# Storing the last tile of a streaming silu-multiply in two pieces of 4 rows instead of four of 2

## The chip, the cores and the metric

The kernel runs on one core of one Trainium2 chip. The metric is device microseconds (us) of one execution; lower is better.

## The reference, cut to what matters

```python
x = randn(32, 512, 2048) float32          # 16384 rows of 2048
x1, x2 = x[..., :1024], x[..., 1024:]
out = (x1 * (1 / (1 + exp(-x1)))) * x2    # silu of one half, times the other half
```

134.22 MB are read and 67.11 MB written.

## The kernel before

There are 16 tiles, numbered 0 to 15 here. A tile is 1024 rows of the input: each of the 128 partitions holds 8 consecutive rows (8 MB in, 4 MB out). Loads are issued by the scalar engine (ACT), stores by the sync engine (SP), so each kind has a queue of its own, and both queues are served by the same 16 DMA engines. An engine moves a transfer in packets; here a packet is the contiguous run of one partition, 64 KB in a load and 32 KB in a store of 8 rows. A queue is said to have drained, or run dry, when the last packet in it is done. Input and output tiles are double-buffered. Compute goes 2 rows at a time: ACT does the silu, the vector engine (DVE) the product.

```python
K = 8                  # rows per partition in a tile
KC = 2                 # rows per compute step
# ...
for i in range(n_tiles):
    # ...
    last = i == n_tiles - 1
    for c in range(0, k, KC):
        ce = min(c + KC, k)
        nc.scalar.activation(out=ot[:, c:ce, :], in_=xt[:, c:ce, :half], func=Silu)
        nc.vector.tensor_mul(out=ot[:, c:ce, :], in0=ot[:, c:ce, :], in1=xt[:, c:ce, half:])
        if last:                                                     # tile 15: one store per step
            nc.sync.dma_start(out=ov[:, c:ce, :], in_=ot[:, c:ce, :])
    if not last:                                                     # tiles 0..14: one store of 8 rows
        nc.sync.dma_start(out=ov, in_=ot[:, :k, :])
    if i + 2 < n_tiles:
        load(i + 2)
```

Of the kernel before, what the change touches and what calls it, by code (L numbers as in the profile page):

```python
# [1 line left out]

# [4 lines left out]


def issue_ahead_of_the_first_barrier(nc):




    head, body = nc.main_func.blocks[:2]
    load = next(ins for ins in body.instructions if type(ins).__name__ == "InstDMACopy")
    at = next(
        j for j, ins in enumerate(head.instructions)
        if ins.engine == load.engine and type(ins).__name__ == "InstDrain"
    )
    body.instructions = [ins for ins in body.instructions if ins.name != load.name]  # L20
    head.instructions = head.instructions[:at] + [load] + head.instructions[at:]


@with_exitstack
def kernel(
    ctx: ExitStack,
    tc: tile.TileContext,
    x: bass.AP,
    out: bass.AP,
):  # L30






    nc = tc.nc
    P = nc.NUM_PARTITIONS

    x_flat = x.flatten_outer_dims()  # L40
    out_flat = out.flatten_outer_dims()
    num_rows, in_cols = x_flat.shape
    half = in_cols // 2
    dt = x_flat.dtype

    K = 8
    KC = 2
    PLAN = [K] * (num_rows // (P * K))

    in_pool = ctx.enter_context(tc.tile_pool(name="in_pool", bufs=2))  # L50
    out_pool = ctx.enter_context(tc.tile_pool(name="out_pool", bufs=2))

    plan = []
    row = 0
    for k in PLAN:
        plan.append((row, k))
        row += P * k
    assert row == num_rows
    n_tiles = len(plan)

    def view(flat, i):
        row0, k = plan[i]
        return flat[row0:row0 + P * k].rearrange("(p k) d -> p k d", k=k)

    nc.at_finalize(issue_ahead_of_the_first_barrier)


    ctx.enter_context(tc.manual_schedule())

    loaded = {}  # L70

    def load(i):
        xt = in_pool.tile([P, K, in_cols], dt, name="xt")
        nc.scalar.dma_start(out=xt[:, :plan[i][1], :], in_=view(x_flat, i))
        loaded[i] = xt

    load(0)
    load(1)
    for i in range(n_tiles):
        k = plan[i][1]  # L80
        xt = loaded.pop(i)
        last = i == n_tiles - 1
        ov = view(out_flat, i)
        ot = out_pool.tile([P, K, half], dt, name="ot")
        for c in range(0, k, KC):
            ce = min(c + KC, k)
            nc.scalar.activation(  # L87
                out=ot[:, c:ce, :],
                in_=xt[:, c:ce, :half],
                func=mybir.ActivationFunctionType.Silu,  # L90
            )
            nc.vector.tensor_mul(  # L92
                out=ot[:, c:ce, :],
                in0=ot[:, c:ce, :],
                in1=xt[:, c:ce, half:],
            )
            if last:
                nc.sync.dma_start(out=ov[:, c:ce, :], in_=ot[:, c:ce, :])
        if not last:
            nc.sync.dma_start(out=ov, in_=ot[:, :k, :])  # L100
        if i + 2 < n_tiles:
            load(i + 2)


# [1 line left out]
_INS = ['x']  # L106
_OUTS = [((32, 512, 1024), 'float32')]


# [23 lines left out]
```

## Time and profile before

| | |
|---|---|
| time before, first three runs | 470.78 us (470.76 to 470.87) |
| span in the profile | 468.9 us |
| moved | 201.35 MB, mean 429 GB/s |
| DVE, ACT busy | 30%, 25% |
| last tile: multiplies end | 455.26, 457.46, 459.67, 461.87 us |
| last tile: stores issued | 455.29, 457.49, 459.69, 461.89 us |
| last data on the DMA engines | 467.62 us |

The page of the kernel before, its totals, the DMA row (busy tenths in 40 slices of the span) and the chain that ended last:

```profile
span 468.9 us, 269 instructions
DVE 142.3 (30%) x64; ACT 118.2 (25%) x65; POOL 0.2 (0%) x4
...
DMA  9899999999999998999999999999999989999998
...
DMA 80%; DVE 15%; ACT 3%; DVEq 0%; issue 0%
```

The DMA engines are at least 80% busy in every slice: they are the bottleneck. Compute appears in the chain because a new load waits for its buffer to be computed, but another load and a store are moving meanwhile.

The end is what the change touches. The timeline of the kernel before (start, duration, engine, line, operation; SPq is the sync engine's queue):

```profile
451.03 7.31 ACT L87 ACTIVATE ot<-xt 128x2048 f32<-128x2048 f32 x4 [21.57 <-DMA xt<-in_x_dram]
452.97 8.90 DVE L92 TENSOR_TENSOR ot<-ot,xt 128x2048 f32<-128x2048 f32 x4 [19.98 <-ACT ot L87]
455.29 6.94 SPq L98 DMA_DIRECT2D out_dram<-ot  x4
```

The four stores of line 98, and the time from issue to landing (minimum, median, maximum):

```profile
L98 SPq DMA_DIRECT2D out_dram<-ot x4: 332/332/333, 455.3 to 461.9; - x4
...
DMA to landing us min/median/max: 5.4/5.7/6.1
```

The windows of the kernel before over its end; the columns to read are the last two, the mean share of the 16 DMA engines and the rate. A packet is counted whole in the window in which it starts, so where packets are as long as the window the shares are lumpy and can exceed 1:

```profile
core 0: us, DVE busy (x) ACT busy (x) POOL busy (x), PEclk, DMA share, GB/s
...
455.00:457.00 2.00, 2.00 (x2) 2.00 (x2) 0.00 (x0) 1.00 0.68 295
457.00:457.50 0.50, 0.50 (x2) 0.50 (x1) 0.00 (x0) 1.00 0.87 361
457.50:458.00 0.50, 0.50 (x1) 0.50 (x1) 0.00 (x0) 1.00 0.97 410
458.00:458.50 0.50, 0.50 (x1) 0.34 (x1) 0.00 (x0) 1.00 1.04 442
458.50:459.00 0.50, 0.50 (x1) 0.00 (x0) 0.00 (x0) 1.00 0.93 393
459.00:467.30 8.30, 2.87 (x2) 0.00 (x0) 0.00 (x0) 1.00 0.97 408
467.30:468.90 1.60, 0.00 (x0) 0.00 (x0) 0.00 (x0) 1.00 0.01 5
```

The engines stay busy from the first small store to the last byte. The trace also records each DMA packet with its start, duration, size and queue. It explains the first two rows: until 457.00 (fastest engine) to 457.81 (slowest) the engines are still moving the whole-tile store of tile 14, in packets of 32 KB and 1.21 us. The first packet of the last tile starts some 3 ns later, on each engine, after a 4-byte completion packet. (The records do not name the engine, but packets of a busy engine follow one another so closely that 16 chains can be told apart.) That store was issued at 455.29, so 1.7 us of its life went by in a queue that was not empty. Its issue costs nothing.

### The profile page before, as it was taken

How to read it: one execution, taken by the hardware profiler on the slowest of the kernel's cores; microseconds unless marked ns; L12 is line 12 of the kernel's file. 1: busy time of each engine (PE TensorE's matmuls, PEld its weight loads, DVE VectorE, ACT ScalarE, POOL GpSimd, SP SyncE). 2: the span in 40 equal slices, each digit the busy share in tenths (PEclk: the TensorE clock that was granted, in tenths of full speed). 3: DMA queues.
4: the chain of work that ended last, by engine and by line, in shares of the span. 5: the costliest groups of instructions: out<-in, count | busy, mean ns of one | idle time of the engine just before them, and what ended most of it. 6: DMA issues, size and time to landing. Idle time of an engine off the chain costs nothing.

```text
span 468.9 us, 269 instructions
## 1 busy us (share of the span) xinstructions
DVE 142.3 (30%) x64; ACT 118.2 (25%) x65; POOL 0.2 (0%) x4
## 2 busy tenths in 40 slices
DVE  0070705106061160601507025070250702407034
ACT  1142406023060330603206032060420604106051
POOL 0000000000000000000000000000000000000000
DMA  9899999999999998999999999999999989999998
GB/s 431 375 447 403 447 447 447 403 419 431 447 447 403 447 492 363 442 492 391 458 403 439 456 447 403 409 442 447 447 403 444 467 386 447 442 419 481 400 409 354
DMA packets 5042, 201.35 MB, mean 429 GB/s; under 512 B 560, under 2 KB 560, under 8 KB 560
## 3 DMA queue, kind: packets, MB, share of 16 engines
q10 hardware_dynamic: 2304, 134.22, 66.4%
q1 hardware_dynamic: 2736, 67.11, 33.2%
q14 instruction: 2, 0.02, 0.0%
HBM read 134.22 MB, written 67.11 MB: 429 GB/s over the span
## 4 chain that ended last, share of the span: by engine, by line
DMA 80%; DVE 15%; ACT 3%; DVEq 0%; issue 0%
DMA xt<-in_x_dram 80%; DVE ot L92 15%; ACT ot L87 3%; DVEq L128 0%
## 5 line engine op out<-in xcount | busy, mean ns | idle before, releaser
L92 DVE TENSOR_TENSOR ot<-ot,xt 128x2048 f32<-128x2048 f32 x64 | 142.3, 2286 | 319.5 <-ACT ot L87 319.5
L87 ACT ACTIVATE ot<-xt 128x2048 f32<-128x2048 f32 x64 | 116.9, 1897 | 338.8 <-DMA xt<-in_x_dram 338.8
L87 ACT ACT_TABLE_LOAD x1 | 1.3, 1283 | 1.3 <-PEq L117 1.3
L117 POOL MEMSET const-uint8-127<- 128x1 uint8 x1 | 0.1, 102 | 0.0
L117 POOL MEMSET const-bfloat16-1.0<- 128x1 bf16 x1 | 0.1, 101 | 0.0
L117 POOL MEMSET const-float32-0.0<- 128x1 f32 x1 | 0.1, 98 | 0.2 <-issue 0.2
L117 POOL MEMSET const-float32-1.0<- 128x1 f32 x1 | 0.1, 98 | 0.0
## 6 DMA issues: line engine op xcount, KB each, us to landing
out_dram<-ot SPq DMA_DIRECT2D x15, 4096.0 KB, 39.8
out_dram<-ot SPq DMA_DIRECT2D x4, 1024.0 KB, 5.7
xt<-in_x_dram ACTq DMA_DIRECT2D x16, 47.1
```

What stands on the lines that cost most here:

```text
L87: nc.scalar.activation(out=ot[:, c:ce, :], in_=xt[:, c:ce, :half], func=mybir.ActivationFunctionType.Silu,)
L92: nc.vector.tensor_mul(out=ot[:, c:ce, :], in0=ot[:, c:ce, :], in1=xt[:, c:ce, half:],)
L117: nc = _bacc.Bacc("TRN2", target_bir_lowering=False, num_devices=1)
```

## The change

The intent is fewer and larger stores: two of 2 MB in place of four of 1 MB. Two issues and two completions fall away, and the contiguous run per partition grows from 8 KB to 16 KB. The computation is untouched.

```diff
     K = 8
     KC = 2
+    KS = 4
@@
-            if last:
-                nc.sync.dma_start(out=ov[:, c:ce, :], in_=ot[:, c:ce, :])
+            if last and ce % KS == 0:
+                nc.sync.dma_start(out=ov[:, ce - KS:ce, :], in_=ot[:, ce - KS:ce, :])
```

## The prediction

> **What bounds the kernel.** Memory traffic. The page's totals give 201.35 MB at 429 GB/s over a span of 468.9 us; its DMA row shows 9 or 8 tenths in every slice; DVE is busy 30%, ACT 25%. The chain of waits is 80% load, and the compute in it (1.92 us ACT, then 8.91 us DVE per tile) runs beside other transfers. The change touches only the end.
>
> **The end, before.** Timeline and store line: the last tile's load is consumed at 451.03; its four multiplies of 2.29 us end 2.20 us apart; each releases a 1 MB store, issued at 455.29, 457.49, 459.69 and 461.89 (0.33 us each). Packet records: tile 14's whole-tile store still has packets in the store queue until 457.0 on the fastest DMA engine and 457.8 on the slowest. The first small store's packets start 0.01 us behind them on each engine: its issue is entirely hidden. From then on the engines have no gap until 467.62 (windows: DMA share 0.97 to 0.98 from 457.5 to 467.3): 32 packets of 8 KB per engine, 0.306 us apart, 9.81 us. The sync queue's wait ends at 467.98 and the closing barrier takes 0.9 us. So the tail is bound by DMA throughput, not by when the last multiply ends.
>
> The Trainium skill, "DMA: Bandwidth & Descriptors", section "Queues, rings and completion order", says that each DMA engine consumes descriptors in ring order; the trace agrees, the last tile's packets following tile 14's.
>
> **What the change does.** The first store of the last tile waits for two multiplies: issue at 457.49 instead of 455.29. The last half's store goes at 461.89 as before. Two issues of 0.33 us vanish from the sync queue, which is idle: worth nothing. Packets become 16 KB instead of 8 KB, 256 instead of 512. From the records, 32 KB packets follow each other every 1.209 us (27.1 B/ns), 8 KB ones every 0.306 us (26.8 B/ns); 16 KB ones should take 0.609 us, 16 per engine 9.74 us: 0.07 us gained.
>
> **What lies on the critical path.** The slack that hides the first issue is smaller than 2.20 us. Issue to first packet was 1.01 us for the very first load (engines idle), most engines within 0.26 us of the first; the first small store bounds it at 1.71 us, since its packets were there by then. So piece one starts at 458.5 to 459.2, where the store queue ran dry at 457.0 to 457.8: the slowest engine idles some 0.7 to 1.5 us. Piece two, issued at 461.89, is queued by 463.6 at the latest, and piece one lasts until about 463.4 to 464, so no second gap, or a tiny one. The end moves by the gap less 0.07 us: about +0.9 us, all in the last slice.
>
> Predicted: 471.7 us, 8 times in 10 between 471.0 and 472.7. Faster by over 2%: 0.01; within 2%: 0.98; slower by over 2%: 0.01.
>
> **What would show it.** Two stores on the store line, issued near 457.5 and 461.9; windows with DMA share well under 1 between about 457.2 and 458.8 (before: 0.87 to 0.98); then gapless until about 468.4; 16 KB packets of about 0.61 us; everything before 455 unchanged.
>
> **What would make it wrong.** A shorter issue latency, or tile 14's store ending later, so nothing is lost; 16 KB packets distinctly faster; longer set-up for the larger store; a second gap before piece two; or earlier stages interleaving differently by some tenths of a per cent, which would drown 0.9 us.

## The result, and the profile after

| | before | after |
|---|---|---|
| median of 6 runs | 470.89 us | 471.53 us |
| lowest to highest | 470.76 to 471.38 | 471.31 to 471.74 |
| span in the profile | 468.87 us | 469.54 us |
| first small store issued | 455.29 | 457.57 |
| its first packet | 457.00 | 458.40 |
| last data on the DMA engines | 467.62 | 468.40 |

The ratio is 1.0012 with a 95% interval of 0.9999 to 1.0025: the same by the 2% rule, and by the times alone barely told from 1. A ratio here is the mean time of one kernel's fast runs over that of the other's of the same rounds, so it is not quite the ratio of the medians quoted. The difference of the medians is 0.64 us.

The page after:

```profile
span 469.5 us, 265 instructions
DVE 142.3 (30%) x64; ACT 118.2 (25%) x65; POOL 0.2 (0%) x4
...
DMA  9999999999999998999999999999999999999998
...
DMA 80%; DVE 15%; ACT 3%; DVEq 0%; issue 0%
```

Nothing shows at this scale. The timeline after, and its store line:

```profile
451.11 7.31 ACT L88 ACTIVATE ot<-xt 128x2048 f32<-128x2048 f32 x4 [21.18 <-DMA xt<-in_x_dram]
453.05 8.90 DVE L93 TENSOR_TENSOR ot<-ot,xt 128x2048 f32<-128x2048 f32 x4 [19.59 <-ACT ot L88]
457.57 4.74 SPq L99 DMA_DIRECT2D out_dram<-ot  x2
```

```profile
L99 SPq DMA_DIRECT2D out_dram<-ot x2: 332/332/332, 457.6 to 462.0; - x2
...
DMA to landing us min/median/max: 6.3/6.6/6.8
```

Compute starts within 0.08 us of where it did, and the first store is issued 2.28 us later. The windows after:

```profile
core 0: us, DVE busy (x) ACT busy (x) POOL busy (x), PEclk, DMA share, GB/s
...
455.00:457.00 2.00, 2.00 (x2) 2.00 (x2) 0.00 (x0) 1.00 0.87 377
457.00:457.50 0.50, 0.50 (x2) 0.50 (x1) 0.00 (x0) 1.00 0.01 0
457.50:458.00 0.50, 0.50 (x2) 0.50 (x1) 0.00 (x0) 1.00 0.01 0
458.00:458.50 0.50, 0.50 (x1) 0.42 (x1) 0.00 (x0) 1.00 1.00 426
458.50:459.00 0.50, 0.50 (x1) 0.00 (x0) 0.00 (x0) 1.00 0.23 98
459.00:467.30 8.30, 2.94 (x2) 0.00 (x0) 0.00 (x0) 1.00 1.04 442
467.30:468.90 1.60, 0.00 (x0) 0.00 (x0) 0.00 (x0) 1.00 0.39 164
```

From 457.0 to 458.0 no data packet starts: the shares that were 0.87 and 0.97 are 0.01. (The 0.23 in the fifth row is only lumpiness: the packets of 0.61 us that started just before 458.5 are counted in the row above.) By the packet records tile 14's store ends at 457.11 to 457.89, and the first packets of the last tile start together at 458.40 to 458.55. Each engine has a hole of between 0.51 us (last end to first start) and 1.44 us (first end to last start). Across a hole the 16 chains cannot be told apart: holes per engine are bounds. The tail's work, about 9.8 us per engine, is nearly unchanged but starts later, and it is what 467.30 to 468.90 now contains.

The two profiles account for the difference of 0.67 us in the span. The first issue came 2.28 us later (2.20 by the change, 0.08 because the last load happened to land later in this run). The time from the first issue to the last data shrank by 1.51 us, from 12.34 to 10.83 us: the last engine to start waited 0.98 us from the issue to its first packet where it had been 2.53 us, and its transfer took 0.04 us longer. The close-out, from the last data to the end of the span, shrank from 1.25 to 1.14 us. The sum is 2.28 - 1.51 - 0.11 = 0.66 us, the rest rounding.

### The profile page after: what moved, and what is told of

It reads as the page before. It is cut to its first block, busy times and chain, and to the rows that moved or that the text cites. A ratio compares the mean times of both kernels' runs of the same rounds, so it can differ in the third digit from the quotient of the medians.

```text
span 469.5 us, 265 instructions
## 1 busy us (share of the span) xinstructions
DVE 142.3 (30%) x64; ACT 118.2 (25%) x65; POOL 0.2 (0%) x4
## 4 chain that ended last, share of the span: by engine, by line
DMA 80%; DVE 15%; ACT 3%; DVEq 0%; issue 0%
DMA xt<-in_x_dram 80%; DVE ot L93 15%; ACT ot L88 3%; DVEq L129 0%
```

## The experiments

The theory to be tested, called the gap theory: the DMA engines bind the tail, so a late issue costs exactly what exceeds the time for which the store queue is still busy. The rivals: the size of the stores or packets costs the time; the larger last store costs it; or the 0.64 us is drift. All times are medians; "over before" is the difference to the median of before. Kernels are compared only within the same rounds.

| run | last tile's stores (rows) | over before, us | 95% interval of the ratio |
|---|---|---|---|
| e0_after | 4, 4 | +0.61 | 0.9999 to 1.0024 |
| e1_late4 (failed to delay) | 2, 2, 2, 2 | -0.30 | 0.9984 to 1.0009 |
| e9_late4_held | 2, 2, 2, 2, in pairs | +0.63 | 0.9998 to 1.0023 |
| e2_422 | 4, 2, 2 | +0.94 | 1.0007 to 1.0034 |
| e3_224 | 2, 2, 4 | +0.04 | 0.9988 to 1.0013 |
| e4_62 | 6, 2 | +2.77 | 1.0045 to 1.0072 |
| e5_8 | 8 | +4.94 | 1.0091 to 1.0118 |
| e10_26 | 2, 6 | +2.37 | 1.0035 to 1.0063 |
| e6_rows1_ks4 | 4, 4, computed by single rows | +0.06 | 0.9992 to 1.0017 |
| e7_prev_small | 4, 4, tile 14 in 2-row stores | +0.30 | 0.9993 to 1.0018 |
| e7b_prev_small_2222 | 2, 2, 2, 2, tile 14 likewise | +0.31 | 0.9991 to 1.0016 |
| e8_rows1_ks1 | eight of 1, computed by single rows | +0.14 | 0.9986 to 1.0012 |

### e0_after: the change again

No edit.

> The changed kernel again, on the chip that the next three runs use. Gap theory (the store queue runs dry before the first 4-row piece's packets come; the trace has them 0.83 us after the issue at 457.57): +0.5 to +0.9 us over before. Noise theory (the 0.64 us of the first comparison is drift, its interval holds 1): a ratio not told from 1, sign changing from round to round.

Measured: 471.67 us against 471.06, +0.61 us; the ratio is again 1.0012. Its interval again just holds 1, so the times alone did not rule drift out; the hole is there again in the packet records, 0.40 to 1.9 us per engine.

### e1_late4: a delay that was none

In the changed kernel:

```diff
-                nc.sync.dma_start(out=ov[:, ce - KS:ce, :], in_=ot[:, ce - KS:ce, :])
+                for s in (ce - KS, ce - KC):
+                    nc.sync.dma_start(out=ov[:, s:s + KC, :], in_=ot[:, s:s + KC, :])
```

> Timing alone: four 2-row stores as before (8 KB packets), but the first is issued together with the second, after the second multiply. Gap theory: the same loss as the changed kernel, +0.5 to +0.9 us over before, with a hole of about 0.5 to 1.4 us per DMA engine near 457.1 to 458.5. Size theory (two larger stores, larger packets or fewer completions cost the time): no loss, +0.0 +- 0.2 us.

Measured: -0.30 us. That looks like a point for the size theory, but the trace shows that the experiment did not do what it was meant to. The store line of e1_late4:

```profile
L100 SPq DMA_DIRECT2D out_dram<-ot x4: 332/332/333, 455.2 to 461.8; - x4
```

The first store was still issued at 455.2. The loop sets it down after the second multiply in the program, but the sync engine runs a stream of its own and waits only for the data that the store reads, rows 0 and 1. So this kernel behaves as the kernel before, and is good only as a gauge of noise: two kernels with the same timing differed by 0.30 us in the median.

### e9_late4_held: the timing alone

In the changed kernel:

```diff
-                nc.sync.dma_start(out=ov[:, ce - KS:ce, :], in_=ot[:, ce - KS:ce, :])
+                for s in (ce - KC, ce - KS):
+                    nc.sync.dma_start(out=ov[:, s:s + KC, :], in_=ot[:, s:s + KC, :])
```

The one difference to e1_late4 is the order. The sync queue runs in order, so the store of rows 0 and 1 now stands behind one that needs the second multiply.

> The timing alone, mended: four 2-row stores, and of each pair the second half is put first into the sync queue, so that the first half really waits behind it for the second multiply (in the run e1_late4 the first store waited for its own rows only and was issued at 455.22 as before, so nothing was delayed). Gap theory: first issue near 457.5, last data 10.8 us later, a hole of 0.5 to 1.9 us per engine, +0.5 to +0.9 us over before, though all packets are 8 KB and all stores 1 MB. Size theory: +0.0 +- 0.2 us.

Measured: +0.63 us, as in the change, with four stores of 1 MB and 8 KB packets as before. One of the 11 runs of before was at 472.82 us, which raises the mean in the ratio but not the median. The store line and the windows of e9_late4_held:

```profile
L100 SPq DMA_DIRECT2D out_dram<-ot x4: 332/379/547, 457.7 to 462.4; - x4
```

```profile
457.00:457.50 0.50, 0.50 (x1) 0.50 (x1) 0.00 (x0) 1.00 0.01 0
457.50:458.00 0.50, 0.50 (x2) 0.50 (x1) 0.00 (x0) 1.00 0.00 0
458.00:458.50 0.50, 0.50 (x1) 0.50 (x1) 0.00 (x0) 1.00 0.16 66
458.50:459.00 0.50, 0.50 (x1) 0.00 (x1) 0.00 (x0) 1.00 1.11 459
```

The hole and the loss come from the issue time. Size, packet length and number of stores are not needed for them. (The two stores of a pair are also reversed here; the packet records show no second hole from that.)

### e2_422 and e3_224: is it the first piece or the last?

Both are edits of the kernel before; the map says which piece ends at which row.

```diff
+    CUTS = {4: 0, 6: 4, 8: 6}     # e2_422;  e3_224: {2: 0, 4: 2, 8: 4}
@@
-            if last:
-                nc.sync.dma_start(out=ov[:, c:ce, :], in_=ot[:, c:ce, :])
+            if last and ce in CUTS:
+                s = CUTS[ce]
+                nc.sync.dma_start(out=ov[:, s:ce, :], in_=ot[:, s:ce, :])
```

> Pieces of 4, 2 and 2 rows. Gap theory: the same hole before the first piece, so +0.5 to +0.9 us, although the last piece is 2 rows again. Rival (the last store is too large, so what is left after the last multiply takes longer): back to before, +0.0 +- 0.2 us.

> Pieces of 2, 2 and 4 rows: the first two as before, the last as in the change. Gap theory: no hole at 457; the first two pieces last until 461.9 (fastest engine) to 462.7 (slowest), the third's packets come at 461.9 + 0.83 = 462.8, so a hole of 0.1 to 0.9 us there and the end +0.1 to +0.4 us. Last-piece theory: the full +0.5 to +0.9 us.

Measured: with the large piece first, +0.94 us; with the large piece last, +0.04 us. The larger last store is not what costs. e2_422 is just above the expected range. In its profiled run the last tile's compute started at 451.63, 0.6 us later than in the profile of before, and from first issue to last data it took 10.90 us, the change 10.83; so that run's excess is mostly a late load, though one profile does not say how often that happened in the timed ones.

e3_224 came out under its expected +0.1 to +0.4 us. Its hole is there: the second piece drained at 462.1 to 462.8 depending on the engine, the third's packets came at 462.8 to 463.0, with up to 0.90 us lost per engine. But the span ends with the engine that is done last, and most of each hole only used up the lead of an engine that had drained early: the last to drain did so at 462.82, and all 16 had restarted by 462.97, at most 0.15 us later. From first issue to last data it took 12.51 us against 12.34. What is left is too small for these timings.

### e4_62, e5_8 and e10_26: larger doses

The edit of e2_422 with other maps:

```diff
+    CUTS = {6: 0, 8: 6}           # e4_62;  e5_8: {8: 0};  e10_26: {2: 0, 8: 2}
```

> Pieces of 6 and 2 rows: a larger dose of the same delay. Gap theory: first issue 459.77, first packets 460.6, then 9.8 us of transfer on each engine: end 2.8 to 3.1 us later than before, about 473.8 us. Last-piece theory: no loss, as the last piece is 2 rows. A cost per piece or per size alone would stay under 1 us.

> One store of all 8 rows. Gap theory: issue 461.97, first packets 462.8, end +4.9 to +5.2 us, about 476 us (slope of one: each us of issue delay past the slack costs one us). If the loss were the completion of the larger last store only, it would grow by the piece's size in a way not tied to the issue time.

> Pieces of 2 and 6 rows: the first issued as early as before, the second after the last multiply. Gap theory: no hole at 457, but the first piece drains at 459.4 to 460.3 and the second's packets come at 461.9 + 0.83 = 462.7, a hole of 2.4 to 3.3 us per engine; then 7.4 us of transfer; +2.4 to +2.9 us. Rival (only the time of the first issue counts, as it alone has to be hidden): +0.0 +- 0.2 us.

Measured: +2.77, +4.94 and +2.37 us. The rule "delay of the first issue less 1.51 us of slack", with both numbers from the two profiles above, gives 2.20 - 1.51 = 0.69 us for the change, 4.41 - 1.51 = 2.90 for e4_62 and 6.60 - 1.51 = 5.09 for e5_8. Measured were 0.64, 2.77 and 4.94. For the change this only restates its own profile, from which the 1.51 was read; for the other two it is a forecast that came true. So past the slack each microsecond of delay costs one, and nearly nothing else enters. In the kernels whose first store was a large one and met a drained queue (in e6_rows1_ks4 on all engines but one), the time from first issue to last data is nearly constant: 10.83 us in the change, 10.82 in e0_after, 10.90 in e2_422, 10.83 in e4_62, 10.83 in e6_rows1_ks4, 10.74 in e5_8. In e9_late4_held, with 8 KB packets, it is 11.02, and in the kernel before 12.34.

e10_26 issues its first store as early as before (455.65) and still loses, 0.03 us less than the expected range. The windows of e10_26:

```profile
459.50:460.50 1.00, 1.00 (x2) 0.00 (x0) 0.00 (x0) 1.00 0.24 98
460.50:461.50 1.00, 1.00 (x1) 0.00 (x0) 0.00 (x0) 1.00 0.00 0
461.50:462.50 1.00, 0.73 (x1) 0.00 (x0) 0.00 (x0) 1.00 0.00 0
```

The hole has moved behind the first piece. It is not the first issue that matters in itself; the queue must not run dry anywhere.

### e6_rows1_ks4: the same stores, ready sooner

In the changed kernel:

```diff
-        for c in range(0, k, KC):
-            ce = min(c + KC, k)
+        kc = 1 if last else KC
+        for c in range(0, k, kc):
+            ce = min(c + kc, k)
```

> Still two pieces of 4 rows, but the last tile is computed one row at a time, so four rows should be ready some 0.8 us sooner (estimate: ACT of one row about 1.04 us, multiplies about 1.14 us apart; first issue near 456.7). Gap theory: first packets near 457.6, so the hole shrinks to 0 to 0.5 us on the fastest engines and to nothing on the slowest: +0.0 to +0.2 us over before. Size theory: the loss stays at +0.5 to +0.9 us.

Measured: +0.06 us, with both 2 MB stores left in. With steps of one row the pipeline of ACT and DVE fills sooner, and four rows are ready 5.7 us after the compute starts (451.33 to 457.05) in place of 6.4 (451.11 to 457.54). The timeline of e6_rows1_ks4:

```profile
451.33 7.68 ACT L89 ACTIVATE ot<-xt 128x1024 f32<-128x1024 f32 x8 [21.43 <-DMA xt<-in_x_dram]
452.42 9.17 DVE L94 TENSOR_TENSOR ot<-ot,xt 128x1024 f32<-128x1024 f32 x8 [18.99 <-ACT ot L89]
457.08 4.88 SPq L100 DMA_DIRECT2D out_dram<-ot  x2
```

The hole shrank to 0 to 0.81 us per engine, none on the engine that drained last.

### e7_prev_small and its control: the same stores behind a different neighbour

```diff
-        if not last:
+        if i == n_tiles - 2:
+            for s in range(0, k, KC):
+                nc.sync.dma_start(out=ov[:, s:s + KC, :], in_=ot[:, s:s + KC, :])
+        elif not last:
             nc.sync.dma_start(out=ov, in_=ot[:, :k, :])
```

e7_prev_small has this in the changed kernel, e7b_prev_small_2222 in the kernel before. As e1_late4 taught, these four stores are issued as their rows become ready, not "at once" as the expectation says.

> Last tile stored exactly as in the change, two pieces of 4 rows. Only tile 14's store differs: four stores of 2 rows (8 KB packets) issued at once in place of one of 8 rows (32 KB packets). If the DMA engines take turns between the two queues by packet, the last load (64 KB packets) gets a larger share beside it and lands 1 to 4 us before 450.6; the last tile is computed sooner and the first 4-row piece is queued before tile 14's store has drained. Gap theory: no hole, +0.0 +- 0.2 us over before with the changed store left in. Size theory: +0.5 to +0.9 us stays.

> The control of e7_prev_small: tile 14 stored in four pieces of 2 rows there as here, but the last tile in four pieces of 2 rows as before. Gap theory: neither has a hole, so the two agree within 0.2 us and what e7 was over before (+0.3 us) belongs to tile 14's smaller packets. Size theory: this one is at before, 0.3 us or more under e7.

Measured: +0.30 and +0.31 us. The timeline of e7_prev_small:

```profile
449.48 7.31 ACT L88 ACTIVATE ot<-xt 128x2048 f32<-128x2048 f32 x4 [19.66 <-DMA xt<-in_x_dram]
...
455.95 4.73 SPq L99 DMA_DIRECT2D out_dram<-ot  x2
```

Compute starts 1.5 us earlier than in the kernel before, the first 4-row store is queued at 455.95, and the packet records have no hole. With that, 4, 4 costs the same as 2, 2, 2, 2. The 0.3 us that both are over before, just outside what was expected of e7_prev_small, must belong to what they share, tile 14's small stores; it is not told from the noise (both intervals hold 1, and the two runs are of different calls).

### e8_rows1_ks1: the other way

```diff
-        for c in range(0, k, KC):
-            ce = min(c + KC, k)
+        kc = 1 if last else KC
+        for c in range(0, k, kc):
+            ce = min(c + kc, k)
```

This is in the kernel before, so it makes eight stores of one row.

> The other way: the last tile computed and stored one row at a time, eight stores of 512 KB with 4 KB packets, the first issued near 453.3. Gap theory: the store queue is busy until 457 anyway, so an earlier issue gains nothing: +0.0 to +0.3 us (estimate: the 8 KB packets ran 0.306 us apart and 32 KB ones 1.209 us, so some 5 ns per packet, 4 KB packets add about 0.15 us). Rival (smaller pieces always end sooner, because less is left after the last multiply): -0.5 us or more.

Measured: +0.14 us by the medians, a ratio of 0.9999. The first store is issued at 453.75 and waits for the same drain at 457 to 458. Once the queue never empties, smaller pieces have nothing left to gain. No run beat the kernel before by more than the noise (e1_late4, with the same timing, was 0.30 us under it).

## Why the prediction was right

**The bottleneck.** It said that the tail is bound by DMA throughput and not by the end of the last multiply. Right: e5_8, e4_62 and e10_26 lose by the length of the hole, e8_rows1_ks1 gains nothing from an earlier issue, and the last multiply ends at nearly the same time in all kernels with 2-row steps and an unchanged tile 14 (461.80 to 462.52).

**The later issue, less the slack.** Right in kind, shown by e9_late4_held (the delay alone gives the loss) and e6_rows1_ks4 and e7_prev_small (the large stores without the delay do not). It put the loss at 0.9 us; measured were 0.64 and, in the repeat, 0.61.

**The term that was mis-sized.** From issue to first packet it allowed 1.0 to 1.7 us, the lower figure from the first load of the kernel. Measured were 0.83 us to the first engine's packet and 0.98 to the last engine's. With these the last engine starts at 457.49 + 0.98 = 458.47, where in the kernel before the last queue ran dry at 457.81: a loss of 0.66 us. Two smaller terms, below, were also missed: the transfer took 0.04 us more where 0.07 us less was forecast, and the close-out took 0.11 us less where nothing was forecast. That these two misses, 0.11 us each, cancel is luck.

**The 16 KB packets.** It expected 0.07 us of gain. There was none: 16 KB packets took 0.618 us on average in the change, and the last tile's 16 took 9.84 us on the mean engine; the 32 small ones of before took 9.81. Where there is no hole the gain is there: in e7_prev_small packets of the same size took 0.611 us, and in e6_rows1_ks4 the one engine without a hole moved its 16 in 9.73 us, the other 15 in 9.82 to 9.87. In e9_late4_held too, the packets after the hole were slower, 0.316 us against 0.309 before. Why packets run 1 to 2% slower after a hole is open. The length of the hole is not it: in e3_224 every engine slowed (0.619 us on average), also those whose hole was at most 0.15 us. The engines start in step there, which may have to do with it, but no run tested that.

**The saved issues and completions.** It called the two issues worth nothing. The issues themselves are worth nothing: they sit on an idle queue. But the close-out was 0.11 us shorter (1.25 to 1.14 us). In the trace the sync engine waits for the completion counts in a fixed order; in the kernel before two more waits, 0.064 us each with their spacing, stood behind the one that ended last, in the change none. The other kernels with 2-row steps and an unchanged tile 14 that store the last tile in several pieces agree: 1.25 to 1.27 us with two waits behind, 1.21 with one, 1.14 to 1.15 with none.

**No second gap.** Right: the second piece was issued at 461.97 with the first still moving until about 463.4, and on no engine do the packet records have a pause of over 0.01 us after the hole.

**The noise.** It feared that a difference of 0.9 us would drown. It nearly did: the interval of each comparison of the change alone holds 1. That the loss is real rests on the repeat and e9_late4_held, on the larger doses, and on the hole in the packet records.

## What to carry to other kernels

In a tail that is bound by DMA, ask of each store not how large it is but whether it is queued before the one ahead of it has drained: cut the first pieces so small that their issue, plus the 0.8 to 1.0 us to the first packet seen here, falls inside the drain of what is already queued. Past that point finer pieces gained nothing here (e8_rows1_ks1), and short of it each microsecond of delay cost one. When an experiment is to delay an instruction, check in the trace that it was delayed: on another engine, program order alone does not do it.

## What the Trainium skill lacked or had wrong

- "DMA: Bandwidth & Descriptors", section "Latency and other measured facts", gives a first byte after about 600 ns for stores and loads issued as here. On drained engines the first packet started 0.83 us after the start of the issuing instruction, which itself took 0.33 us (so 0.50 us after its end). The page does not say from where it counts.
- The same page, section "Bandwidth", advises at least 1 MiB per DMA and lists 1 MB at 341 GB/s, 78% of peak, measured for loads issued from GpSimd. In the kernel before four queued stores of 1 MB moved 4 MB in 9.81 us, 428 GB/s (4,194,304 bytes over 9.81 us). What the page lacks is the state of the queue: here the loss belonged to an empty queue, not to the size, as the same 1 MB stores issued late lost 0.63 us (e9_late4_held).
- The same page, section "Queues, rings and completion order", says that a DMA engine takes turns between queues packet by packet. The trace agrees: near the end 64 KB load packets and 32 KB store packets alternate. What the page does not spell out is that a load's completion has to wait its turn as well. In the kernel before the slowest engine's last load packet ended at 449.34 and its completion packet started at 450.55, one 32 KB store packet of 1.21 us between them; with tile 14's store in 8 KB packets (e7_prev_small) it was 448.75 and 449.05, 0.30 us. This let the last tile's compute start 1.5 us earlier: 0.91 us by the shorter wait, the rest by the load's own earlier end.
- No page has that packets after a common restart of the 16 engines ran slower: 0.618 us against 0.611 us for 16 KB, the third packet of each engine most of all (0.635 to 0.652 us in the change). Its cause is open.
